# A two-layer hybrid encoder: table steps at even distances, and gate projections moved between the attention heads

## Chip, core and metric

The kernel runs on one core of a Trainium2 chip. TensorE (PE in the rows) multiplies, VectorE (DVE), ScalarE (ACT) and GpSimd (POOL) do the element-wise work, SyncE (SP) only issues transfers. Each engine works through its own instructions in order and waits for the others by semaphores. The metric is the device time of one execution, in microseconds (us).

## What is computed

T = 512 tokens, D = 1024, two layers, all in float32. Each layer is, cut to what matters here:

```python
h = rms_norm(x, norm_mix_g[i])
q, k, v, u_f, u_s, gates = split(h @ w_in[i])        # 8 heads of 128; gates: 3 x 1024
y_a = (rms_norm(diff_attention(q, k, v), subln) * c) @ w_attn_br[i]
y_b = fourier_mix(u_f) @ w_fourier_br[i]
z   = gelu(s5_mix(u_s, ...)) @ w_glu[i] + b_glu[i]   # s5: a diagonal state space, both directions
y_c = z[..., :D] * sigmoid(z[..., D:])
g   = sigmoid(gates)
x = x + (g[:, :D]*y_a + g[:, D:2*D]*y_b + g[:, 2*D:]*y_c) @ w_out[i]
h = rms_norm(x, norm_ffn_g[i]);  up = h @ w_up[i]
x = x + (gelu(conv3(up[:, :F])) * up[:, F:]) @ w_down[i]           # F = 22 * 128
x = x + sigmoid(rms_norm(x) @ w_ple_gate[i]) * (p[i] @ w_ple[i])
```

## The kernel before

Activations lie feature-major: a tile holds 128 features by 512 tokens (256 KB in float32). Every product keeps float32 accuracy by a split: each operand is a high part in a reduced format and a low part with the rest, and three matmuls (hi·hi, lo·hi, hi·lo) make one product (`mm`, L106). A weight matrix of 1024 x 128 is a "unit": SyncE loads 512 KB into `wr` (two buffers), ScalarE copies the high part into `wh` (L94), VectorE subtracts to get the low part `wl` (L95), and TensorE does 24 matmuls of 128x512 on it into one of the PSUM tiles `w`. One such unit, multiplied by 1/rms (L626) and put through tanh, is a gate tile (`gate`): m = 32 to 39 gate the attention branch, 40 to 47 the Fourier branch, 48 to 55 the S5 branch.

A layer (`i` = 0 is layer 1) is written as a sequence of stages, and a list scheduler turns the whole program into one instruction order for each engine: what is written first has priority, and what is written later moves ahead into places where an engine would wait. `tc.high_priority(offset=-LOW)` puts a part behind all the rest.

- Norm, then the projection of `u_s` to DRAM (`usd`) and the Fourier mixing.
- Eight heads: `v_pair` for every second head, `qk_proj` for q and k, and `head` (scores, softmax, transposes, product with v, in two halves of the queries; then the head's own norm). In layer 1 the tables of the S5 stage are made between them at low priority (`s5_tables`, one call for each of eight chunks): complex products on GpSimd (L243 to L248, L413 to L433), sums on VectorE (L415, L434), transposing matmuls on TensorE (L425) with copies on ScalarE, and the results go to DRAM (`tab`, `dtab`).
- Eight `s5_chunk`: load the chunk's tables `tb` (1.5 MB, two buffers, L660), 16 matmuls `pv` into `s` (L678), a chain over ScalarE, GpSimd and VectorE with a scan (L683 to L695) that leaves `z`, 24 matmuls `py` into `t` (L701 to L704), and a store of the result `ye` to DRAM (`ysd`). Behind the chunks the gates 32 to 39 and w_attn, then w_four with gates 40 to 47, then gates 48 to 55 (`gc8`) are written; the scheduler puts their matmuls between those of the chunks.
- `s5_out`: 32 loads of 32 KB from `ysd` into `yt` (L716), gelu, split into `soh` and `sol`. These feed w_glu (`s<-soh`), then the branches are merged and w_out follows.
- Feed-forward: 22 turns `f` of one unit "up" (L976, convolution, gelu) and one unit "gate" (product `uu` on GpSimd, L988), then eight output tiles `k` of w_down with 66 matmuls each (L1006). In layer 1 the tables of layer 2 are made here: `steps` is a generator with nine steps (`s5_steps`), and `next(steps)` writes one step, the GpSimd products of one chunk and the matmuls of the chunk before. Which turns call it is written out by hand.
- The gated per-layer embedding (PLE). Layer 2 has no table work; its tables were made in layer 1's feed-forward.

Of the kernel before, what the change touches and what calls it, by code (L numbers as in the profile page):

```python
# [21 lines left out]
L = 2  # L22
NH = 8
KT = 8
# [26 lines left out]
class Kernel:  # L51
# [504 lines left out]
        nc.scalar.activation(z[64:128, 1], ra[64:128], AF.Copy)  # L556
        return a, z

    def head(self, ap, q, k, v, e, nl, gs, bank="m"):

        nc = self.nc
        V = nc.vector
        kk, kl = k
        vh, vl = v
        o = self.ps("o")
        s1 = self.t(ap, "s1", (P, 4), bufs=2)
        s2 = self.t(ap, "s2", (P, 4), bufs=2)
        for half in range(2):
            hs = self.t(ap, "ath", (P, 4, 256), F32R, bufs=2)
            ls = self.t(ap, "atl", (P, 4, 256), F32R, bufs=2)  # L570
            for qi in range(2):
                qs = slice((half * 2 + qi) * P, (half * 2 + qi + 1) * P)
                mx = self.t(ap, "mx", (P, 2), bufs=3)
                qt = half * 2 + qi
                ss = []
                for c in range(2):
                    s = self.ps("s")
                    nc.tensor.matmul(s, lhsT=q[:, c, qs], rhs=kk[:, c], start=True, stop=False)
                    nc.tensor.matmul(s, lhsT=q[:, c, qs], rhs=kl[:, c], start=False, stop=True)  # L579
                    V.tensor_reduce(mx[:, c:c + 1], s, op=ALU.max, axis=AX.X, negate=True)  # L580
                    ss.append(s)
                pr = []
                for c in range(2):
                    pt = self.t(ap, f"pr{c}", bufs=2)
                    nc.scalar.activation(pt, ss[c], AF.Exp, bias=mx[:, c:c + 1],  # L585
                                         accum_out=(s1, s2)[c][:, qt:qt + 1])
                    pr.append(pt)

                c2 = self.t(ap, "c2", (P, 1), bufs=3)
                V.reciprocal(c2, s2[:, qt:qt + 1])  # L590
                V.tensor_scalar(out=c2, in0=c2, scalar1=s1[:, qt:qt + 1], scalar2=nl, op0=ALU.mult, op1=ALU.mult)
                V.scalar_tensor_tensor(out=pr[0], in0=pr[1], scalar=c2, in1=pr[0], op0=ALU.mult, op1=ALU.add)  # L592
                at = self.ps("t")
                for kt in range(4):
                    nc.tensor.transpose(at[:, kt * P:(kt + 1) * P], pr[0][:, kt * P:(kt + 1) * P], self.ident)
                self.split(at.rearrange("p (k q) -> p k q", k=4), hs[:, :, qi * P:(qi + 1) * P],
                           ls[:, :, qi * P:(qi + 1) * P])
            oh = o[:, half * 256:half * 256 + 256]
            n = 0
            for vv, aa in ((vh, hs), (vl, hs), (vh, ls)):  # L600
                for kt in range(4):
                    nc.tensor.matmul(oh, lhsT=vv[kt][:, e * P:(e + 1) * P],  # L602
                                     rhs=aa[:, kt],
                                     start=(n == 0), stop=(n == 11))
                    n += 1

        osb = self.t(ap, "osb", bufs=1)
        og = self.t(ap, "og", bufs=1)
        nc.scalar.activation(osb, o, AF.Square)
        nc.scalar.activation(og, o, AF.Copy)  # L610
        V.scalar_tensor_tensor(out=s1, in0=s1, scalar=EPS, in1=s1, op0=ALU.mult, op1=ALU.mult)
        _, pb = self.rms(osb, P, s1, bank)
        V.tensor_tensor(out=og, in0=og, in1=pb, op=ALU.mult)
        h = self.t(self.op, "oh", dt=F32R, bufs=NH)
        l = self.t(self.op, "ol", dt=F32R, bufs=NH)
        self.split(og, h, l, scale=gs)
        return h, l

    def gate(self, pool, i, m, hh, hl, rb):

        nc = self.nc
        w = self.unit(self.a["w_in"][i, m])
        ps = self.ps_w()
        self.mm(ps, w, hh, hl)
        ga = self.t(pool, "ga", bufs=4)
        nc.vector.tensor_tensor(out=ga, in0=ps, in1=rb, op=ALU.mult)  # L626
        nc.scalar.activation(ga, ga, AF.Tanh, scale=0.5)
        return ga


# [158 lines left out]
    def layer(self, i, x):  # L789
# [5 lines left out]
        hh, hl, rc, rb = self.norm(x, V_GMIX)  # L795
# [12 lines left out]
        nlam, gsub = self.t(rp, "nlam", (P, 1)), self.t(rp, "gsub", (P, 1))  # L808
# [30 lines left out]
        ap = self.pool(f"att{i}")  # L839

        kz = [self.t(aq, f"kz{n}", (P, 2, T), F32R) for n in range(2)]
        for z in kz:
            G.memset(z[64:128, 0].bitcast(F32), 0.0)
            G.memset(z[0:64, 1].bitcast(F32), 0.0)
        v = None
        oh, ol = [], []
        for h in range(NH):
            if h % 2 == 0:
                v = self.v_pair(i, ap, h // 2, hh, hl, rc)
            q = self.qk_proj(i, ar, aq, h, "q", hh, hl, cosr, sinr)  # L850
            k = self.qk_proj(i, ar, aq, 8 + h, "k", hh, hl, cosr, sinr, kz[h % 2])
            if i == 0:
                with tc.high_priority(offset=-LOW):
                    for ch in ([0, 1] if h == 0 else [h + 1] if h < 7 else []):
                        for _ in self.s5_tables(i, ch, "mmmm", tc.tile_snap_priority() - LOW):
                            pass
            r = self.head(ap, q, k, v, h % 2, nlam, gsub, "t" if h >= 7 else "m")
            oh.append(r[0])
            ol.append(r[1])
        if i == 0:  # L860
# [14 lines left out]
        for k in range(KT):  # L875
            ga = ga8[k]
# [14 lines left out]
        for k in range(KT):  # L891
            if k % 2 == 0:
                w = self.unit(a["w_four"][i, k // 2])
            ps = self.ps_w()
            self.mm(ps, w[(k % 2) * 4:(k % 2) * 4 + 4], fh, fl)
            ga = self.gate(ge if k < 4 else gt, i, 40 + k, hh, hl, rb)
            V.scalar_tensor_tensor(out=ga, in0=ga, scalar=1.0, in1=ps, op0=ALU.add, op1=ALU.mult)
            G.tensor_tensor(out=m[k], in0=m[k], in1=ga, op=ALU.add)
        gc8 = [self.gate(ge if k < 4 else gt, i, 48 + k, hh, hl, rb) for k in range(KT)]
        s5.release()  # L900
        sp = self.pool(f"so{i}")
        gl = self.pool(f"gl{i}")
# [68 lines left out]
        for f in range(NF):  # L971
# [14 lines left out]
            u = self.t(ff, "uu", bufs=2)  # L986
            V.tensor_tensor(out=u, in0=ps, in1=rb, op=ALU.mult)
            G.tensor_tensor(out=u, in0=u, in1=c, op=ALU.mult)  # L988
            if i + 1 < L and f in (8, 10, 13, 15, 18, 20):
                next(steps)  # L990
            h = self.t((fa, fb)[f // half], "ah", dt=F32R, bufs=half)
            l = self.t((fa, fb)[f // half], "al", dt=F32R, bufs=half)
# [3 lines left out]
        for k in range(KT):  # L996
            w = []
            for c in range(0, NF, 8):
                n = min(8, NF - c)
                w.append(self.unit(a["w_down"][i, k, :, c * P:(c + n) * P], cols=n * P))  # L1000
            ps = self.ps_w()
            c = 0
            for b, u in enumerate(w):
                self.mm(ps, u, ah[c:c + len(u)], al[c:c + len(u)], start=(b == 0), stop=(b == len(w) - 1))
                c += len(u)
            V.tensor_tensor(out=x[k], in0=ps, in1=x[k], op=ALU.add)  # L1006
            if i + 1 < L and k in (0, 1, 3):
                next(steps)
        fb.release()
        fa.release()  # L1010
# [267 lines left out]
```

## Time and profile before

| | |
|---|---|
| three runs | 2200.38, 2203.23 (median), 2203.36 us |
| profiled execution | 2204.09 us; its span from first to last instruction 2202.1 us |
| TensorE busy | 2104.7 us, 96% of the span |
| VectorE, ScalarE, GpSimd busy | 1499.7, 1014.8, 714.0 us |
| mean granted TensorE clock | 0.980 of full speed |

A busy TensorE is counted from the start of a matmul to its modelled end, and matmuls overlap, so what one matmul costs is read from long runs of them in the chain of waits. The granted clock of a stretch is a mean over its time: where the clock is low, the engine runs at 1.2 instead of 2.4 GHz. Where a view gives a line such as L106 for many matmuls, the tile names tell them apart (`w<-hh,wh` is a matmul of the weight's high part by the activation's high part `hh` into `w`).

### The profile page before, as it was taken

The page shows a single profiled execution, that of the slowest core. Times are in us where ns is not written, and L with a number is a line of the kernel's source. Part 1 is how long each engine was busy: PE and PEld are TensorE (multiplying, and loading weights), DVE is VectorE, ACT ScalarE, POOL GpSimd, SP SyncE. Part 2 cuts the span into 40 slices and gives each one's busy share as a digit, 9 for nine tenths or more (in the row PEclk, how much of TensorE's full clock was granted, in tenths as well). Part 3 has the DMA queues.
Part 4 walks back from the last instruction along what each step waited for, and adds up shares of the span by engine and source line. Part 5 has one row for each costly group of instructions (what it writes and reads, how often), then busy time and mean ns, then how long its engine had stood idle before and what let it go on. Part 6 is the DMA issues. An engine that isn't in the chain of part 4 may idle for free.

```text
span 2202.1 us, 28732 instructions
## 1 busy us (share of the span) xinstructions
PE 2104.7 (96%) x10432; PEld 1770.9 (80%) x10432; DVE 1499.7 (68%) x2497; ACT 1014.8 (46%) x1900; POOL 714.0 (32%) x618
## 2 busy tenths in 40 slices
PE   8799889899999999989999999999999999999998
PEld 6778778788888787777888988787888888888886
DVE  7988898366567988785467588764666666665344
ACT  4266656244434443333244577652444444444333
POOL 4488786023002337686112333201320011110000
PEclk9899999999999999989999999999999999999999
DMA  5233223765323244345534312126743333333341
GB/s 193 75 109 100 82 99 123 193 206 196 116 91 98 77 145 138 124 137 160 175 117 154 103 56 58 58 68 160 251 156 104 95 96 96 96 96 98 98 129 58
DMA packets 119038, 263.37 MB, mean 120 GB/s; under 512 B 44369, under 2 KB 50513, under 8 KB 116721
## 3 DMA queue, kind: packets, MB, share of 16 engines
q1 hardware_dynamic: 102672, 247.84, 35.6%
q10 hardware_dynamic: 16224, 13.70, 2.6%
q8 instruction: 82, 1.34, 0.2%
q14 instruction: 60, 0.48, 0.1%
HBM read 218.97 MB, written 42.47 MB: 119 GB/s over the span
## 4 chain that ended last, share of the span: by engine, by line
PE 65%; DVE 9%; POOL 5%; DMA 4%; ACT 3%; issue 1%; ACTq 0%; DVEq 0%; SPq 0%; POOLq 0%
PE w L106 49%; PE s L106 5%; DVE wl L95 2%; PE w L1139 1%; PE s L678 1%; DMA tab<-tb 1%; DMA U<-usd 1%; PE o L602 1%; DMA fraw<-fd 1%; PE w L1086 1%; PE w L1088 1%; PE w L1087 1%; PE t L704 1%; PE t L701 1%; PE t L702 1%
## 5 line engine op out<-in xcount | busy, mean ns | idle before, releaser
L95 DVE TENSOR_TENSOR wl<-wr,wh 128x512 fp32r<-128x512 f32 x596 | 478.6, 809 | 242.2 <-ACT wh L94 238.5
L106 PE MATMUL w<-hh,wh 128*128 128x512 f32 x1536 | 608.7, 397 | 23.4 <-DVE rs L538 7.7
L106 PE MATMUL w<-hl,wh 128*128 128x512 f32 x1536 | 605.1, 394 | 2.6 <-DVE hl L82 2.5
L106 PE MATMUL w<-hh,wl 128*128 128x512 f32 x1536 | 604.8, 394 | 0.0
L94 ACT ACTIVATE wh<-wr 128x512 fp32r<-128x512 f32 x596 | 365.2, 623 | 516.4 <-PE w L106 357.0
L106 PEld LDWEIGHTS w<-hh,wh 128*128 128x128 f32 x1536 | 291.8, 190 | 89.2 <-DVE rs L538 9.5
L106 PEld LDWEIGHTS w<-hl,wh 128*128 128x128 f32 x1536 | 291.8, 190 | 64.1 <-DVE hl L82 4.9
L106 PEld LDWEIGHTS w<-hh,wl 128*128 128x128 f32 x1536 | 291.2, 190 | 60.6 <-DVE wl L95 0.2
L988 POOL TENSOR_TENSOR uu<-uu,cv 128x512 f32<-128x512 f32 x44 | 70.5, 1602 | 287.6 <-DVE cv L198 287.6
L186 POOL TENSOR_TENSOR sq<-sq,sq 128x512 f32<-128x512 f32 x18 | 25.3, 1404 | 352.5 <-ACT sq L184 352.4
L106 PE MATMUL w<-ah,wh 128*128 128x512 f32 x352 | 138.5, 393 | 0.0
L106 PE MATMUL w<-ah,wl 128*128 128x512 f32 x352 | 138.2, 392 | 0.0
L106 PE MATMUL w<-al,wh 128*128 128x512 f32 x352 | 137.2, 390 | 0.0
L585 ACT ACTIVATE pr<-s,mx 128x512 f32<-128x512 f32 x128 | 88.0, 690 | 36.5 <-DVE mx L580 35.8
L580 DVE TENSOR_REDUCE mx<-s 128x1 f32<-128x512 f32 x128 | 85.6, 681 | 22.5 <-PE s L579 22.1
L539 POOL TENSOR_TENSOR rs<-rs,sinr 128x512 f32<-128x512 f32 x32 | 48.1, 1503 | 106.1 <-DVE rs L538 93.5
L112 POOL TENSOR_TENSOR rsq<-rmv,mhalf 128x4 f32<-128x4 f32 x22 | 25.6, 1166 | 169.1 <-DVE rmv L145 98.4
L106 PEld LDWEIGHTS w<-ah,wl 128*128 128x128 f32 x352 | 66.4, 189 | 14.7
L106 PEld LDWEIGHTS w<-al,wh 128*128 128x128 f32 x352 | 66.4, 189 | 14.1
L106 PEld LDWEIGHTS w<-ah,wh 128*128 128x128 f32 x352 | 66.4, 189 | 13.5
L106 PE MATMUL w<-oh,wh 128*128 128x512 f32 x128 | 51.8, 410 | 10.0 <-ACT wh L94 10.0
L592 DVE SCALAR_TENSOR_TENSOR pr<-pr,c,pr 128x512 f32<-128x512 f32 x64 | 59.7, 933 | 1.4
(422 smaller groups left out, 4152.7 us busy)
## 6 DMA issues: line engine op xcount, KB each, us to landing
wr<-in_w_in SPq DMA_DIRECT2D x112, 512.0 KB
wr<-in_w_up SPq DMA_DIRECT2D x88, 512.0 KB
tb<-tab SPq DMA_DIRECT2D x16, 1536.0 KB
tab<-tb SPq DMA_DIRECT2D x64, 256.0 KB
wr<-in_w_down SPq DMA_DIRECT2D x32, 512.0 KB
tab<-vbt SPq DMA_DIRECT2D x32, 256.0 KB
wr<-in_w_attn SPq DMA_DIRECT2D x16, 512.0 KB
wr<-in_w_glu SPq DMA_DIRECT2D x16, 512.0 KB
```

The source lines that it names most:

```text
L94: nc.scalar.activation(hi[:, :n], raw[:, c:c + n], AF.Copy)
L95: nc.vector.tensor_tensor(out=lo[:, :n], in0=raw[:, c:c + n], in1=hi[:, :n].bitcast(F32), op=ALU.subtract)
L106: nc.tensor.matmul(ps, lhsT=w[i][a], rhs=b[i], start=start and i == 0 and q == 0, stop=stop and i == n - 1 and q == 2)
L112: self.nc.gpsimd.tensor_tensor(out=y, in0=v, in1=self.mhalf[:, :n], op=ALU.pow)
L186: eng.tensor_tensor(out=sq, in0=sq, in1=acc[c], op=ALU.add)
L539: nc.gpsimd.tensor_tensor(out=rs, in0=rs, in1=sinr, op=ALU.mult)
L580: V.tensor_reduce(mx[:, c:c + 1], s, op=ALU.max, axis=AX.X, negate=True)
L585: nc.scalar.activation(pt, ss[c], AF.Exp, bias=mx[:, c:c + 1], accum_out=(s1, s2)[c][:, qt:qt + 1])
L592: V.scalar_tensor_tensor(out=pr[0], in0=pr[1], scalar=c2, in1=pr[0], op0=ALU.mult, op1=ALU.add)
L602: nc.tensor.matmul(oh, lhsT=vv[kt][:, e * P:(e + 1) * P], rhs=aa[:, kt], start=(n == 0), stop=(n == 11))
L678: nc.tensor.matmul(pv[:, c0:c0 + NC], lhsT=tb[:, d, g * P:(g + 1) * P], rhs=u, start=True, stop=True)
L988: G.tensor_tensor(out=u, in0=u, in1=c, op=ALU.mult)
```

## The change

Two things. First, the turns of the feed-forward loop that call `next(steps)`: six turns and three output tiles become five turns and four output tiles. Second, in layer 1 alone, the 16 gates 40 to 55 are no longer computed behind the heads. `gate_out` computes gate 40 + 2h ahead of head h and gate 41 + 2h between the halves of head h, in the one buffer that the head's squared output `osb` also uses, and stores the tile to DRAM (`gd`) on ScalarE's queue. Where the gate is used, `gate_in` loads it back into a `ga` tile on SyncE's queue. Gates 32 to 39 and all of layer 2 stay.

```diff
-    def head(self, ap, q, k, v, e, nl, gs, bank="m"):
+    def head(self, ap, q, k, v, e, nl, gs, bank="m", between=None):
@@ end of the loop over the two halves
+            if half == 0 and between is not None:
+                between()
@@ gate
-    def gate(self, pool, i, m, hh, hl, rb):
+    def gate(self, pool, i, m, hh, hl, rb, tag="ga", bufs=4):
...
-        ga = self.t(pool, "ga", bufs=4)
+        ga = self.t(pool, tag, bufs=bufs)
...
+    def gate_out(self, pool, i, m, hh, hl, rb):
+        ga = self.gate(pool, i, m, hh, hl, rb, "osb", 1)
+        self.gd[m] = self.t(self.dp, f"gd{m}")
+        self.nc.scalar.dma_start(self.gd[m], ga)
+
+    def gate_in(self, pool, i, m, hh, hl, rb):
+        if m not in self.gd:
+            return self.gate(pool, i, m, hh, hl, rb)
+        ga = self.t(pool, "ga", bufs=4)
+        self.nc.sync.dma_start(ga, self.gd[m])
+        return ga
@@ loop over the heads
-            r = self.head(ap, q, k, v, h % 2, nlam, gsub, "t" if h >= 7 else "m")
+            if i == 0:
+                self.gate_out(ap, i, 40 + 2 * h, hh, hl, rb)
+            r = self.head(ap, q, k, v, h % 2, nlam, gsub, "t" if h >= 7 else "m",
+                          (lambda: self.gate_out(ap, i, 41 + 2 * h, hh, hl, rb)) if i == 0 else None)
@@ merging
-            ga = self.gate(ge if k < 4 else gt, i, 40 + k, hh, hl, rb)
+            ga = self.gate_in(ge if k < 4 else gt, i, 40 + k, hh, hl, rb)
...
-        gc8 = [self.gate(ge if k < 4 else gt, i, 48 + k, hh, hl, rb) for k in range(KT)]
+        gc8 = [self.gate_in(ge if k < 4 else gt, i, 48 + k, hh, hl, rb) for k in range(KT)]
@@ feed-forward
-            if i + 1 < L and f in (8, 10, 13, 15, 18, 20):
+            if i + 1 < L and f in (7, 10, 13, 16, 19):
                 next(steps)
...
-            if i + 1 < L and k in (0, 1, 3):
+            if i + 1 < L and k in (0, 2, 4, 6):
                 next(steps)
```

How this moves the instructions is seen in the engines' orders. TensorE at the last chunk of layer 1's S5 stage (`s<-U` is `pv`, `t<-z` and `t<-U` are `py`, `w<-hh` a gate), before:

```order
L678 MATMUL s_4405<-U_4051,tb_4396 128x64 x8
L106 MATMUL w_5444<-hh_114,wh_5436 128x512
L106 MATMUL w_5444<-hl_115,wh_5436 128x512
L702 MATMUL t_4380<-z_4366,tb_4348 128x63
L704 MATMUL t_4380<-z_4366,tb_4348 128x63
L701 MATMUL t_4380<-U_4051,dr_4352 128x64
L702 MATMUL t_4380<-z_4366,tb_4348 128x63
L704 MATMUL t_4380<-z_4366,tb_4348 128x63
L701 MATMUL t_4380<-U_4051,dr_4352 128x64
L702 MATMUL t_4380<-z_4366,tb_4348 128x63
L704 MATMUL t_4380<-z_4366,tb_4348 128x63
L701 MATMUL t_4380<-U_4051,dr_4352 128x64
```

and in the changed kernel, where line 678 is 693 and lines 701, 702 and 704 are 716, 717 and 719:

```order
L717 MATMUL t_4972<-z_4958,tb_4940 128x63
L719 MATMUL t_4972<-z_4958,tb_4940 128x63
L693 MATMUL s_4997<-U_4691,tb_4988 128x64 x8
L716 MATMUL t_5020<-U_4691,dr_4992 128x64
L693 MATMUL s_5045<-U_4691,tb_5036 128x64 x8
L717 MATMUL t_5020<-z_5006,tb_4988 128x63
L719 MATMUL t_5020<-z_5006,tb_4988 128x63
L716 MATMUL t_5020<-U_4691,dr_4992 128x64
L717 MATMUL t_5020<-z_5006,tb_4988 128x63
L719 MATMUL t_5020<-z_5006,tb_4988 128x63
L716 MATMUL t_5020<-U_4691,dr_4992 128x64
L717 MATMUL t_5020<-z_5006,tb_4988 128x63
```

Between the last two `pv` and behind them there were gate and w_four matmuls; now the chunks' own matmuls stand one after the other. In the whole stretch from the first `pv` to the first `s<-soh`, 528 matmuls of 128x512 have become 193.

ScalarE in the heads, at the norm of the second head's output (`osb`, `og`), before:

```order
L81 ACTIVATE vh_1949<-w_1824,rsq_179 128x256
L609 ACTIVATE osb_1799<-o_1672 128x512
L610 ACTIVATE og_1800<-o_1672 128x512
L426 ACTIVATE vbt_1636<-m_1637 128x256
L427 ACTIVATE kfb_986<-m_1637 128x32
L78 ACTIVATE ath_2116<-t_2135 128x4x128
L585 ACTIVATE pr_505_2189,s_482_2114<-s_2181,mx_2180 128x512
L81 ACTIVATE vh_1953<-w_1824,rsq_179 128x256
L81 ACTIVATE vh_2689<-w_2571,rsq_179 128x256
```

and in the changed kernel (L609 is L611; L629 is a gate's tanh):

```order
L611 ACTIVATE osb_1959<-o_1792 128x512
L612 ACTIVATE og_1960<-o_1792 128x512
L94 ACTIVATE wh_2510<-wr_2504 128x512
L81 ACTIVATE vh_2113<-w_1984,rsq_179 128x256
L94 ACTIVATE wh_2552<-wr_2550 128x512
L94 ACTIVATE wh_2556<-wr_2550 128x512
L629 ACTIVATE osb_2308<-osb_2308 128x512
L636 DMA gd_520_2311<-osb_2308 128x512
L544 ACTIVATE ks_2204<-ra_2198 128x1024
```

A gate's weight copies (L94), its tanh and its store to `gd` have come in behind the head's `osb`, in the same buffer.

ScalarE at the end of layer 1's feed-forward (`dtab` is the last table, `hh` the activation for the next stage, one tile for each output tile `x0` to `x7`), before:

```order
L491 DMA dtab_1484_6692<-kfb_1474_6681 48x512
L491 DMA dtab_1484_6692<-kfb_1474_6681 32x512
L491 DMA dtab_1484_6692<-kfb_1474_6681 16x512
L81 ACTIVATE hh_2191_10181<-x4_1312_5923,vec_7_86 128x512
L94 ACTIVATE wh_2152_9949<-wr_2149_9943 128x512
L78 ACTIVATE ph_2213_10245<-praw_2212_10243 128x512
L94 ACTIVATE wh_2155_9955<-wr_2154_9953 128x512
L78 ACTIVATE ph_2216_10251<-praw_2215_10249 128x512
L94 ACTIVATE wh_2157_9959<-wr_2154_9953 128x512
L94 ACTIVATE wh_2160_9965<-wr_2159_9963 128x512
L94 ACTIVATE wh_2162_9969<-wr_2159_9963 128x256
L81 ACTIVATE hh_2193_10185<-x5_1313_5924,vec_7_86 128x512
```

and in the changed kernel:

```order
L94 ACTIVATE wh_2259_10342<-wr_2256_10336 128x512
L94 ACTIVATE wh_2265_10385<-wr_2264_10383 128x512
L491 DMA dtab_1516_6756<-kfb_1506_6745 128x512
L491 DMA dtab_1516_6756<-kfb_1506_6745 112x512
L491 DMA dtab_1516_6756<-kfb_1506_6745 96x512
L491 DMA dtab_1516_6756<-kfb_1506_6745 80x512
L491 DMA dtab_1516_6756<-kfb_1506_6745 64x512
L491 DMA dtab_1516_6756<-kfb_1506_6745 48x512
L491 DMA dtab_1516_6756<-kfb_1506_6745 32x512
L491 DMA dtab_1516_6756<-kfb_1506_6745 16x512
L81 ACTIVATE hh_2229_10257<-x7_1347_5990,vec_7_86 128x512
```

The `dtab` transfers, which stood ahead of the fifth of the eight `hh`, now stand ahead of the eighth.

## Rows read from the trace of the kernel before

**Rows 1.** the page: busy time by engine; costliest groups, one of them

```profile
PE 2104.7 (96%) x10432; PEld 1770.9 (80%) x10432; DVE 1499.7 (68%) x2497; ACT 1014.8 (46%) x1900; POOL 714.0 (32%) x618
...
L988 POOL TENSOR_TENSOR uu<-uu,cv 128x512 f32<-128x512 f32 x44 | 70.5, 1602 | 287.6 <-DVE cv L198 287.6
```

**Rows 2.** the chain of waits, pieces in order: start us, us, what

```profile
415.40 15.55 DMA U<-usd
...
476.42 1.73 PE s L678 x16
...
501.78 1.79 PE s L678 x16
...
1786.74 346.21 PE w L106 x1522
```

**Rows 3.** stretches: length, busy of PE, PEld, DVE, ACT, POOL, clock, DMA share

```profile
100.00:400.00 300.00, 276.22 (x1562) 238.22 (x1562) 252.69 (x414) 181.48 (x395) 219.58 (x186) 0.97 0.32 106
400.00:446.00 46.00, 38.77 (x168) 31.32 (x166) 14.51 (x25) 10.91 (x20) 1.40 (x2) 0.89 0.82 186
446.00:602.00 156.00, 156.00 (x848) 134.70 (x846) 98.17 (x134) 72.73 (x120) 37.85 (x31) 1.00 0.54 176
1245.00:1500.00 255.00, 249.53 (x1437) 215.91 (x1436) 186.55 (x354) 166.03 (x325) 68.43 (x50) 1.00 0.20 64
```

**Rows 4.** TensorE's waits from 100 to 400 us: total, times, longest

```profile
PE w L106 <- DVE rs L538: 7.0, 3, 3.4
PE m L425 <- DVE tb L415: 3.8, 1, 3.8
```

**Rows 5.** TensorE's waits from 700 to 1106 us

```profile
PE m L425 <- DVE tb L415: 18.6, 3, 7.9
```

**Rows 6.** the feed-forward stage and a stretch in it, columns as in rows 3

```profile
700.00:1106.00 406.00, 381.21 (x1690) 315.07 (x1690) 307.36 (x467) 153.07 (x302) 219.91 (x181) 0.96 0.42 135
880.00:892.00 12.00, 6.35 (x22) 5.67 (x23) 9.24 (x9) 3.10 (x6) 10.77 (x9) 0.57 0.35 109
```

**Rows 7.** first and last mark of the feed-forward stage, layer 1, then 2

```profile
L976 DVE TENSOR_TENSOR gp<-w,rstd x22: 672/679/687, 708.5 to 970.4; 128x512 f32<-128x512 f32 x22
...
L1006 DVE TENSOR_TENSOR x<-w,x x8: 672/682/692, 992.4 to 1105.0; 128x512 f32<-128x512 f32 x8
...
L976 DVE TENSOR_TENSOR gp<-w,rstd x22: 678/693/694, 1787.4 to 2006.7; 128x512 f32<-128x512 f32 x22
...
L1006 DVE TENSOR_TENSOR x<-w,x x8: 690/692/692, 2027.2 to 2133.0; 128x512 f32<-128x512 f32 x8
```

**Rows 8.** the table matmuls: one of four banks; two neighbours in time

```profile
L425 PE MATMUL m<-cat,tb x32: 283/286/580, 816.4 to 1043.3; 128*128 128x144 f32 x32
...
816.36 0.65 PE L425 MATMUL m<-cat,tb 128*128 128x144 f32 x4
816.84 0.65 PE L425 MATMUL o<-cat,tb 128*128 128x144 f32 x4
```

**Rows 9.** VectorE by line, 120 to 360 us, then 2000 to 2100 us

```profile
L95 DVE TENSOR_TENSOR wl<-wr,wh 128x512 fp32r<-128x512 f32 x35 | 42.5, 1224 | 7.5 <-ACT wh L94 7.4
...
L95 DVE TENSOR_TENSOR wl<-wr,wh 128x512 fp32r<-128x512 f32 x33 | 22.9, 693 | 54.3 <-ACT wh L94 54.2
```

**Rows 10.** loads of tb (440 to 560 us); a chunk's first, last link

```profile
L660 SPq DMA_DIRECT2D tb<-tab x6: 326/327/589, 466.8 to 527.3; - x6
...
503.66 0.59 ACT L683 ACTIVATE sw<-s 64x512 f32<-64x512 f32 x1 [1.39 <-PE s L678]
...
511.98 0.68 DVE L695 TENSOR_TENSOR z<-z,sw 128x512 f32<-128x512 f32 x1
```

**Rows 11.** tiles yt, sol and soh from 540 to 640 us

```profile
L716 SPq DMA_DIRECT2D yt<-ysd x32: 574/575/698, 552.6 to 578.3; - x32
...
L106 PE MATMUL s<-soh,wh x53: 387/394/397, 601.5 to 639.8; 128*128 128x512 f32 x53
L82 DVE SCALAR_TENSOR_TENSOR sol<-yg,soh x4: 1089/1098/1106, 568.1 to 585.4; 128x512 fp32r<-128x512 f32 x4
```

More of the change, by code (lines that the diff above doesn't have):

```diff
@@ L845, in layer @@
         v = None
+        self.gd = {}
         oh, ol = [], []
```

## Prediction

> **What bounds the kernel now.** I read the busy table first, then the table by stage, the chain of waits, and TensorE's waits in the stages that the change touches. TensorE is busy 2104.7 of 2202.1 us [rows 1], and one 128x512 matmul of the long runs takes 346.21/1522 = 0.227 us [rows 2]: a 1024x128 projection ("unit", 24 such matmuls) takes 5.45 us. So time can only come from stretches in which TensorE idles or runs at the lower clock, and these are few. In layer 1's attention (100 to 446 us) TensorE idles 23.8 + 7.2 us, and at granted clocks of 0.97 and 0.89 it does about 9 + 5 us less than at full clock: 45 us lost [rows 3]. Layer 2's heads, without table work, lose 5.5 us in 255 [rows 3]. The waits in layer 1 are for VectorE, which in turn follows GpSimd's chains [rows 4], and the stage closes on transfers, the last of them the 15.55 us gather of U [rows 2]. The second place is layer 1's feed-forward stage: from its first to its last mark on VectorE it takes 1105.0 - 708.5 = 396.5 us, layer 2's 2133.0 - 1787.4 = 345.6 us [rows 7]. Of the 50.9 us difference the table matmuls themselves explain 15 (four banks of 32, four matmuls in 816.84 - 816.36 = 0.48 us [rows 8], so 128 x 0.12); 35 are lost: 24.8 idle in 406 us, the rest low clock [rows 6]. The S5 chunk stage (446 to 602) has TensorE full, 156.00 of 156 [rows 3].
>
> **Part 1: table steps in the feed-forward stage.** Nothing is added: nine calls of `next(steps)` stay nine. Over the stage GpSimd is busy 219.91 us [rows 6], of which 22 products `uu` at 1.6 us [rows 1] are 35; the other 185 are eight chunks of tables at 23. With three `uu` beside it a chunk takes 28 us, some 31 with the waits inside its chain. Before, the steps follow each other after 2, 3, 2, 3, 2 turns of up and gate; a turn is two units, 10.9 us of TensorE work, so every other step comes after 21.8, less than GpSimd's 31, and TensorE waits for `tb` 18.6 us in three waits [rows 5]. Around one of them, in 880 to 892, the granted clock is 0.57 [rows 6]. After: every third turn (32.7 us), then every second output tile of w_down (2 x 66 x 0.227 = 30). I take the waits for `tb` as gone, with the lower clock behind them: 32 of the 35 us. What is late next: the last step now comes at k = 6. Its chain (table matmuls, ScalarE's copies, 15 `dtab` transfers on ScalarE's queue) stands ahead of the copy of the last `hh` that the next stage needs, where before four more output tiles' work covered it. I put 5 us on that (0: the 66 matmuls of k = 7, 15 us, cover it; 12: most of the chain's transfers are open). Sum: -32 + 5 = -27 us, bounds -15 (half of the waits stay, since the margins are within 2 us) and -33.
>
> **Part 2: 16 gates moved into the heads.** It takes 16 units from behind the heads and puts them among the heads: 16 x 5.45 = 87 us of TensorE work, none saved. It adds 16 stores of 256 KB on ScalarE's queue and 16 loads on SyncE's, and the weights' 512 KB loads move along. In the attention the DMA engines are busy 0.32 of the time [rows 3], so I cost these at nothing; if that cover were gone, the loads would delay the `tb` behind them on SyncE's queue, which belongs to the second rival.
>
> Heads. In the order, 193 matmuls of 128x512 stand between the first chunk and the first `soh` matmul, where 528 stood: 335 x 0.227 = 76 us of work come ahead of the first chunk and may fill holes. Of the 45 us lost, layer 2's level over 346 us (5.5 x 346/255 = 7.5) is the least that stays: recovery at most 37. At least 10: each unit also needs VectorE (two subtractions, one product, 0.7 us each at best), which is busy 252.69 of 300 us [rows 3], and no unit shortens the transfers at the stage's end. I take 28: GpSimd's 219.58 us would spread over some 350 us instead of 300, a share of 63% instead of 73%, so that its chains are late less often. First chunk: 76 - 28 = 48 us later.
>
> On VectorE the subtraction `wl` takes 1224 ns in the heads, beside GpSimd, and 693 ns late in layer 2, where GpSimd hardly works [rows 9]. The Trainium skill (SBUF — State Buffer, "Who interferes with whom") says that a VectorE instruction with two SBUF inputs contends with a GpSimd instruction that reads SBUF, and that whichever comes second is blocked until the other is through. By that rule, with which the two rows agree, 32 subtractions moved beside GpSimd's tables would cost 32 x 0.53 = 17 us, in part on GpSimd's chains; the third rival has this as a mechanism of its own.
>
> Chunk stage. Before, it is full of work: 528 x 0.227 = 120 us and the chunks' own. A chunk has 16 `pv` matmuls (1.73 us [rows 2]) and 24 `py` matmuls of that size (2.6 us): 35 us for eight. After, 193 x 0.227 + 35 = 79 us are left, and the chunks' chain sets the pace. `tb` has two buffers, so chunk n+2 loads only after chunk n's last matmul. One cycle: the load of `tb` at most 476.42 - 466.8 = 9.6 us [rows 2, 10]; from the start of `pv` to `z` 512.66 - 501.78 = 10.9 [rows 2, 10]; `py` 2.6: 23. Measured for a cycle of two chunks, with other work between the links: 501.78 - 476.42 = 25.4 [rows 2]. From first `pv` to last `py` it was 552.6 - 446 = 107 us [rows 3, 11]. Without other work in the way three cycles of 20 (a load of 6.5, my guess) and 23 for the two ends give 83; between 83 and 107 I take 97, the measured being nearer. Then `s5_out`: 32 loads of `yt` from 552.6 to 578.3, and the last `sol` 8 us later (585.4 + 1.1) [rows 11]: 34 us. After, the 32 stand together on SyncE (32 x 0.575 = 18 us of issue), and most need early chunks alone; between 17 and 34 I take 24. Some `soh` matmuls are through by then (-4), the clock has to come back after holes (+3): 97 + 24 - 1 = 120 us against 156: -36. Before, the gates covered `s5_out`'s 34 us and 15 more up to 601.5 [rows 11]; that cover is gone.
>
> Layer 1 up to the feed-forward: +48 - 36 = +12 (ends: -28, all filled; +35, least recovery and old pace). From the end of layer 1's feed-forward on the order is the same.
>
> **Sum.** +12 - 27 = -15 us on the profiled execution's 2204.09: 2189. The median of the runs is 0.9 us below the profiled execution: 2188.
>
> **Rivals.**
> 1. The fill suffices: no chunk stalls, the stage falls to its 79 us of work: +48 - 76 - 27 = -55, 2148 us. For it: w_attn units stand among the first chunks. Against: in the order the last four chunks have next to nothing between them. 0.11.
> 2. Slower: the chunk chain keeps its old pace without its filler, 107 + 34 = 141 us from first `pv` to the last `sol`, and the heads recover only 16: +60 - 15 - 27 = +18, 2221 us. For it: 25.4 us is nearly the sum of the links with a load of 9.6. With 28 recovered it decides once the stretch passes 135 us (48 - (156 - 135) - 27 = 0). 0.15.
> 3. VectorE and GpSimd hold each other up in the heads: each moved subtraction blocks for its 0.69 us, 32 x 0.69 = 22 of the 28 us recovered are lost: +7, 2210 us. For it: the two means [rows 9]. Against: the rest of the heads' units bear the same already. 0.10.
> 4. Even spacing gains nothing, since GpSimd's 31 us is an average and its chain also waits for transfers: +12 alone, 2215 us. Against: the waits are few, three, and at short distances. 0.04.
>
> **How the numbers follow.** The forecast has 0.60, its own range 2172 to 2206: part 1 between -15 and -33, layer 1 between +2 and +18. The whole range, 2162 to 2216, leaves out rival 1 and the upper part of rival 2. A difference of 0.2% (4.4 us) is about what a measurement of this kernel can tell from no change. Faster: 0.49 of the forecast's 0.60 and rival 1's 0.11, 0.60. Same: 0.08 of the forecast and 0.04 of rival 3, 0.12. Slower: rivals 2 and 4, the rest of 3 and 0.03 of the forecast, 0.28.
>
> **What would show it.** Right: layer 1's feed-forward marks some 27 us closer, hardly a wait for `tb` there; first `pv` near 494 us; TensorE idle 30 to 45 us in the chunk stage, waiting for `z` and for `soh`; first `pv` to first long run of `soh` matmuls near 120 us. Wrong: a chunk stage with TensorE full (rival 1) or over 135 us long (2); a first `pv` after 510 us (3); unchanged waits for `tb` (4).

## The result, and the profile after

The changed kernel is slower: 2234.23 us median (2232.45 to 2235.95) against 2201.92, ratio 1.0146 with a 95% interval of 1.0133 to 1.0158. Forecast was 2188, with a range up to 2216. The profiled execution has a span of 2233.1 us, 31.0 more than before. (Ratios here and below compare runs in the chip's faster state; of all the runs one, of `e11_dummy` below, was not in it: 3051.58 us at a granted clock of 0.651.) First the page: total busy time, and the 40 slices of TensorE's busy share and granted clock.

```profile
PE 2123.8 (95%) x10432; PEld 1776.5 (80%) x10432; DVE 1488.9 (67%) x2497; ACT 1013.8 (45%) x1900; POOL 714.3 (32%) x618
PE   8899999999779999999999999999999999999998
PEclk9899999999679999999999999999999999999999
```

In the 11th and 12th slice (558 to 670 us) TensorE is busy at 7 tenths and the granted clock falls to 6 and 7 tenths: the second half of layer 1's S5 chunk stage and the `soh` matmuls behind it; TensorE was full there before. The table by stage (length, busy of PE, PEld, DVE, ACT, POOL, clock, DMA share):

```profile
100.00:460.00 360.00, 343.02 (x1850) 289.02 (x1849) 270.61 (x456) 204.89 (x436) 221.94 (x186) 0.99 0.37 122
460.00:506.00 46.00, 44.21 (x202) 36.26 (x201) 14.45 (x24) 12.29 (x21) 1.13 (x2) 0.96 0.78 182
506.00:641.60 135.60, 105.34 (x539) 90.09 (x537) 74.71 (x93) 48.30 (x80) 38.49 (x31) 0.78 0.54 179
740.00:1140.00 400.00, 382.66 (x1710) 313.42 (x1709) 303.52 (x450) 153.80 (x302) 217.19 (x181) 0.99 0.43 136
```

Against [rows 3]: from 100 us to the first `pv` it is now 406 us instead of 346, with 18.8 us idle instead of 31. The stage from 506 on is 30 us idle at a clock of 0.78. The marks that bound the stages, by tile and line (the two `soh` numbers come from the chain of waits, next block):

```profile
L693 PE MATMUL s<-U,tb x128: 217/275/472, 505.9 to 600.9; 128*128 128x64 f32 x128
...
L719 PE MATMUL t<-z,tb x64: 275/348/422, 521.9 to 614.5; 128*128 128x63 f32 x64
...
L995 DVE TENSOR_TENSOR gp<-w,rstd x22: 674/680/687, 744.3 to 1001.4; 128x512 f32<-128x512 f32 x22
...
L1025 DVE TENSOR_TENSOR x<-w,x x8: 672/676/692, 1018.3 to 1129.9; 128x512 f32<-128x512 f32 x8
...
L995 DVE TENSOR_TENSOR gp<-w,rstd x22: 680/693/694, 1818.5 to 2037.7; 128x512 f32<-128x512 f32 x22
```

And the chain of waits (start us, us, what):

```profile
480.36 14.30 DMA U<-usd
590.51 7.09 DMA tb<-tab
597.64 3.64 PE s L693 x16
...
641.60 28.84 PE s L106 x120
```

The same marks before, first `pv`, last `py` and the long run of `soh` in the chain:

```profile
L678 PE MATMUL s<-U,tb x128: 217/275/276, 445.5 to 539.0; 128*128 128x64 f32 x128
...
L704 PE MATMUL t<-z,tb x64: 275/275/275, 461.2 to 552.4; 128*128 128x63 f32 x64
...
601.69 32.98 PE s L106 x144
```

These marks account for the difference (the feed-forward marks of before stand in [rows 7]):

| stage of layer 1 | before | after | difference | forecast |
|---|---|---|---|---|
| up to the first `pv` | 445.5 | 505.9 | +60.4 | +48 |
| first `pv` to the long run of `soh` matmuls | 156.2 | 135.7 | -20.5 | |
| from there to the first feed-forward mark | 106.8 | 102.7 | -4.1 | -36 with the row above |
| feed-forward, first to last mark | 396.5 | 385.6 | -10.9 | -32 |
| from there to layer 2's first feed-forward mark | 682.4 | 688.6 | +6.2 | +5 |
| sum | | | +31.1 | -15 |

Every gain that was forecast came with the right sign, but smaller: 16 us in the heads for 28, 25 in the chunk stage for 36, 11 in the feed-forward for 32. Of the 46 us between forecast and result, the feed-forward is 21, the heads 12, the chunk stage 11 and the end of the feed-forward 1. What TensorE waits for now, in the heads (100 to 460), the chunk stage (505 to 645) and the feed-forward (730 to 1150), total us, times, longest:

```profile
PE s L578 <- ACT pr L585: 8.3, 13, 1.4
...
PE s L106 <- ACT soh L81: 14.8, 4, 8.8
PE t L717 <- DVE z L710: 8.6, 4, 3.6
PE s L693 <- DMA tb<-tab: 3.8, 1, 3.8
...
PE w L106 <- DVE gp L995: 9.6, 5, 4.9
PE w L106 <- ACT ge L197: 2.9, 2, 1.6
PE w L106 <- ACT ah L81: 2.5, 1, 2.5
```

The feed-forward's 18.6 us for `tb` [rows 5] is gone, as forecast, and the three waits shown last, 15.0 us, stand there instead. Two of them were there before as well, with 3.3 us (`gp` 1.8, `ge` 1.5); all of TensorE's waits between the first and the last mark fall from 24.6 us to 15.8. The longest, in order of time, on GpSimd, VectorE and TensorE (start us, us, engine, line; in brackets the idle time before it and what ended it):

```profile
911.72 1.51 POOL L247 TENSOR_TENSOR tb<-pt 128x512 f32<-128x512 f32 x1
913.31 1.63 POOL L248 TENSOR_TENSOR tb<-tb,tb 128x512 f32<-128x512 f32 x1
...
917.14 1.05 POOL L414 TENSOR_TENSOR tb<-pt,bc 128x512 f32<-128x512 f32 x1
918.15 1.26 POOL L1007 TENSOR_TENSOR uu<-uu,cv 128x512 f32<-128x512 f32 x1
...
911.53 0.78 DVE L198 SCALAR_TENSOR_TENSOR cv<-ge,cv 128x512 f32<-128x512 f32 x1
...
918.23 1.73 DVE L415 TENSOR_TENSOR tb<-tb,tb 128x512 f32<-128x512 f32 x1 [2.75 <-POOL tb L414]
920.11 1.31 DVE L82 SCALAR_TENSOR_TENSOR al<-uu,ah 128x512 fp32r<-128x512 f32 x1
921.35 0.68 DVE L995 TENSOR_TENSOR gp<-w,rstd 128x512 f32<-128x512 f32 x1
...
922.17 0.76 PE L106 MATMUL w<-hh,wh 128*128 128x512 f32 x1 [4.87 <-DVE gp L995]
```

The gelu's result `cv` is there at 912.3 (911.53 + 0.78), but the product `uu` starts on GpSimd at 918.15, behind the table products L247 to L414 in its queue. `al` on VectorE follows it, `gp` stands behind `al` in VectorE's queue and frees TensorE's PSUM tile only at 922: 4.87 us idle. But ahead of `al` in VectorE's queue stands a table sum (L415), which waits 2.75 us for GpSimd's L414 and ends at 919.96, while `al` has its operands at 920.08 (ScalarE's copy `ah` of `uu`): without the late `uu`, `al` would have begun only some 0.15 us earlier. So here two results of GpSimd's queue are late together, and the table sum alone would have held `gp`. The same order, L414, L415, `al`, `gp`, stands ahead of the waits for `gp` that end at 882 and 962.

### The profile page after: what moved, and what is told of

It is laid out like the page before. It is cut to its first block, busy times and chain, and to the rows that moved or that the text cites. A ratio compares the mean times of both kernels' runs of the same rounds, so it can differ in the third digit from the quotient of the medians.

```text
span 2233.1 us, 28798 instructions
## 1 busy us (share of the span) xinstructions
PE 2123.8 (95%) x10432; PEld 1776.5 (80%) x10432; DVE 1488.9 (67%) x2497; ACT 1013.8 (45%) x1900; POOL 714.3 (32%) x618
## 4 chain that ended last, share of the span: by engine, by line
PE 69%; DVE 11%; POOL 7%; DMA 5%; ACT 4%; issue 3%; SPq 1%; ACTq 1%; DVEq 0%; POOLq 0%
PE w L106 50%; PE s L106 5%; PE w L1158 3%; DVE wl L95 2%; PE o L602 1%; PE s L693 1%; DMA U<-usd 1%; DMA tab<-tb 1%; PE s L578 1%; PE s L579 1%; PE t L595 1%; PE t L719 1%; PE t L717 1%; POOL uu L1007 1%; PE w L1105 1%
## 5 line engine op out<-in xcount | busy, mean ns | idle before, releaser
L95 DVE TENSOR_TENSOR wl<-wr,wh 128x512 fp32r<-128x512 f32 x596 | 470.9, 796 | 238.7 <-ACT wh L94 235.6
L94 ACT ACTIVATE wh<-wr 128x512 fp32r<-128x512 f32 x596 | 364.5, 622 | 494.6 <-PE w L106 348.5
L106 PEld LDWEIGHTS w<-al,wh 128*128 128x128 f32 x352 | 66.1, 188 | 14.6 <-DVE al L82 0.5
L106 PE MATMUL s<-soh,wh 128*128 128x512 f32 x128 | 51.5, 408 | 15.2 <-ACT soh L81 14.8
L578 PE MATMUL s<-ks,qs 128*128 128x512 f32 x128 | 54.3, 432 | 10.0 <-ACT pr L585 9.6
```

Of the source, the lines that this page charges most:

```text
L94: nc.scalar.activation(hi[:, :n], raw[:, c:c + n], AF.Copy)
L95: nc.vector.tensor_tensor(out=lo[:, :n], in0=raw[:, c:c + n], in1=hi[:, :n].bitcast(F32), op=ALU.subtract)
L106: nc.tensor.matmul(ps, lhsT=w[i][a], rhs=b[i], start=start and i == 0 and q == 0, stop=stop and i == n - 1 and q == 2)
```

## The experiments

All are timed against the kernel before on the same chip. Where stage times are given, they are read from the same marks as in the table above.

**The two parts alone.** `e1_spacing` is the kernel before with the two lines of the feed-forward changed; `e2_gates16` is the changed kernel with these two lines put back.

> The kernel before with the new table turns alone (gates stay behind the heads). Theory S, the two parts add up stage by stage as the marks of the changed kernel say: feed-forward marks of layer 1 closer by 11 us (385.6 instead of 396.5), then 6 us lost again up to layer 2, so 5 us less than before, 2197. Rival: the part of the changed kernel's feed-forward that is still lost comes from what the moved gates did before it, and the spacing alone brings the full 27 us, 2175. Second rival: the spacing brings nothing by itself, 2202.

> The changed kernel with the old table turns: the 16 gates alone. Theory S: first pv 60 us later, first pv to the long soh run 20 us shorter, 4 us won behind it: 36 us more than before, 2238. Rival: the gates cost less than that and the turns cost part of the 31 us: under 2225.

Measured: 2195.72 us, ratio 0.997 (0.9962 to 0.9979), and 2241.78, ratio 1.0177 (1.0164 to 1.0191). Together -0.3% and +1.8% make the +1.5% of both, so the parts add up, theory S. The spacing is worth 7 us, the gates cost 39.

How far marks of two single executions can be told apart: in `before`, `e1_spacing`, `e4_uu` and `e8_uu_old`, whose code up to the first `pv` is the same, it starts at 445.5, 443.8, 442.7 and 441.5 us. A difference of 4 us at that mark therefore shows little.

**How many gates, and where.** `e3_gates8` moves eight, one ahead of each head, with the old turns:

```diff
-                self.gate_out(ap, i, 40 + 2 * h, hh, hl, rb)
+                self.gate_out(ap, i, 40 + h, hh, hl, rb)
...
-                          (lambda: self.gate_out(ap, i, 41 + 2 * h, hh, hl, rb)) if i == 0 else None)
+                          None)
```

> Eight gates (40 to 47, one ahead of each head) pass through DRAM instead of 16, the eight gates 48 to 55 stay behind w_four; old table turns. Theory H, the heads have few holes that a gate fits into, so about a fifth of the moved work is recovered, and the chunk chain keeps its 107 us whatever filler it has: first pv later by 35 (8 x 5.45 less a fifth), the stage from first pv to the soh run 135 to 141 us instead of 156: 15 to 20 us more than before, 2217 to 2222. Rival C, the loss is the starved chunk stage alone: eight gates are enough filler for s5_out's 34 us, the heads fill their holes (28 of 44 us recovered): same as before or faster, 2190 to 2202.

Measured: 2214.28 us, ratio 1.0051 (1.0036 to 1.0066), between the two forecasts and nearer to H's. The first `pv` comes 23.8 us later (469.3). How much work has moved ahead of it is counted as in the prediction, by the matmuls that start before it. From the start to the first `pv`, before, here and in `e2_gates16` (columns as in the table by stage, matmuls in the first bracket):

```profile
0.00:445.40 445.40, 392.34 (x2116) 334.50 (x2117) 350.43 (x650) 229.24 (x492) 270.77 (x253) 0.95 0.40 122
```

```profile
0.00:469.20 469.20, 425.34 (x2284) 358.88 (x2285) 356.79 (x669) 241.41 (x513) 269.35 (x253) 0.98 0.41 129
```

```profile
0.00:506.20 506.20, 464.53 (x2451) 389.96 (x2452) 370.72 (x694) 254.87 (x536) 273.81 (x253) 0.98 0.42 131
```

Eight gates are 43.6 us of work, but 24 matmuls of w_attn that ran ahead of the first `pv` before now come behind it: 168 more matmuls, 38.1 us at 0.227. So 14 us are recovered (the work moved ahead less the delay), more than H's fifth and less than C's two thirds. With 16 gates it is 335 matmuls, 76 us, for 60.8 us, 15 recovered: the second eight added about nothing. From the first `pv` to the long run of `soh` matmuls it takes 146.0 us (615.3 - 469.3), 10 less than before (theory H: 15 to 21), and to the first feed-forward mark 14 less. The eight chunks themselves, first `pv` to last `py`, take 118.6 us, longer than the 107 that H wanted to stay; why they are longer stays open:

```profile
L693 PE MATMUL s<-U,tb x128: 217/275/276, 469.3 to 572.7; 128*128 128x64 f32 x128
...
L719 PE MATMUL t<-z,tb x64: 275/275/421, 483.9 to 587.9; 128*128 128x63 f32 x64
```

`e5_between8` puts the same eight between the halves, `e9_ahead16` all 16 ahead of the heads, two at a time; both with the old turns.

> Eight gates (40 to 47) again, but each between the halves of its head instead of ahead of it; old table turns. With the eight ahead of the heads the first pv came 24 us later for 43.6 us of moved work; with all 16 it came 61 later for 76. Theory P, the place: a gate between the halves recovers nothing, it only lengthens the head: first pv 36 to 44 us later than before, total 12 to 20 us over the run with eight ahead, 2226 to 2234. Rival N, the number: the heads hold some 20 us of room whatever the place, and eight gates use it up: first pv again about 24 us later, total 2212 to 2217.

> All 16 gates, two ahead of each head and none between its halves; old table turns. Theory P: first pv 48 us later than before or less (half of 76 recovered, and more), total below 2230. Rival N: first pv about 60 us later as in the changed kernel, total 2238 to 2243.

Measured: 2223.03, ratio 1.0101 (1.0087 to 1.0114), first `pv` 28.5 us later; and 2239.27, ratio 1.0173 (1.0159 to 1.0187), first `pv` 58.7 later. With eight gates the first `pv` lies between the two theories and nearer to N, with 16 it is as N says. The work moved ahead is again 168 matmuls in the one and 328 in the other, so 10 and 16 us are recovered. So it is mainly the number: the heads have room for 10 to 16 us. The place shows 5 us at this mark with eight gates and 2 with 16, about what marks of single executions scatter. In the whole time the eight between the halves are 10 us slower than the eight ahead (6 above N's range, 3 below P's), which the first `pv` explains only in part; with 16 the place makes no difference.

**GpSimd's queue in the feed-forward.** `e4_uu` is `e1_spacing` with layer 1's products `uu` on VectorE, `e8_uu_old` the same edit with the old turns:

```diff
-            G.tensor_tensor(out=u, in0=u, in1=c, op=ALU.mult)
+            (V if i + 1 < L else G).tensor_tensor(out=u, in0=u, in1=c, op=ALU.mult)
```

> As the run with the new turns alone, and layer 1's 22 products uu go to VectorE instead of GpSimd. Theory Q, in the changed kernel the products uu wait behind the table products in GpSimd's queue, al behind them and gp behind al on VectorE, so TensorE's waits for gp, ge and ah (15 us) go with this: 8 to 12 us less than the new turns alone, about 2187. Rival V, VectorE itself is the bound there (304 of 400 us busy): 22 x 0.7 = 15 us more on it, no gain or a loss against the new turns alone, 2197 to 2210.

> The kernel before with uu of layer 1 on VectorE alone, old turns. Theory Q: uu waits in GpSimd's queue with either table of turns, but with the old turns TensorE waits for the table matmuls' tb first (18.6 us), which needs GpSimd's speed; GpSimd has 35 us less to do, so part of this goes too: 5 to 10 us less than before, 2192 to 2197. Rival: without uu on GpSimd the old turns are as good as the new ones, 2180 to 2185. Second rival: no change, 2202.

Measured: 2182.50 us, ratio 0.9912 (0.9899 to 0.9926), and 2190.28, ratio 0.9956 (0.9944 to 0.9969). Theory Q holds: 13 us less than the new turns alone, although VectorE has more to do. With the old turns the edit gives 11, a little over what Q expected. The new turns are worth 9 us on top of this edit, each against its own runs of the kernel before, and were worth 7 without it. The waits of TensorE in the new turns without and with the edit (700 to 1110 us, total, times, longest):

```profile
PE w L106 <- DVE gp L976: 7.5, 5, 2.8
PE w L106 <- ACT ge L197: 4.5, 3, 1.6
PE w L106 <- ACT ah L81: 2.5, 1, 2.5
```

```profile
PE w L106 <- DVE gp L976: 6.4, 4, 2.6
```

The waits for `ge` and `ah` are gone and that for `gp` hardly less (7.5 to 6.4), which theory Q had wrong in part; the marks from first to last are 372.0 us apart instead of 386.6. VectorE's own waits in the same stretch, without and with the edit, show both halves:

```profile
DVE tb L415 <- POOL tb L414: 26.0, 8, 7.3
DVE al L82 <- ACT ah L81: 17.2, 14, 2.0
```

```profile
DVE tb L415 <- POOL tb L414: 32.8, 8, 8.6
...
DVE al L82 <- ACT ah L81: 0.9, 2, 0.7
```

The wait of `al` for `ah`, ScalarE's copy of `uu`, is gone: that was the late `uu`. The table sums L415 still wait for GpSimd, and the two longest waits for `gp` that are left, 2.6 and 2.5 us, end behind such sums in VectorE's queue. Between the two marks TensorE idles 6.5 us instead of 16.4.

**What paces the chunks.** In `e2_gates16`, with hardly any filler, first `pv` to last `py` took 109 us, in the kernel before 107. Two runs start from `e2_gates16` (all 16 gates moved, old turns). `e10_halftb` loads half of each table and has four buffers for it; the products with the other half take the first half's rows instead, so this kernel leaves that part of the result out:

```diff
-        tb = self.t(pool, "tb", (P, 6, 512), bufs=2)
-        nc.sync.dma_start(tb, tab.rearrange("p (k x) -> p k x", k=6))
+        tb = self.t(pool, "tb", (P, 3, 512), bufs=4)
+        nc.sync.dma_start(tb, tab.rearrange("p (k x) -> p k x", k=6)[:, 0:3])
...
```

`e11_dummy` adds 42 matmuls that keep TensorE running:

```diff
+        if self.gd and ch < 7:
+            with self.tc.high_priority(offset=-LOW):
+                dm = self.ps("o")
+                for r in range(6):
+                    nc.tensor.matmul(dm, lhsT=U[:, 0:2].rearrange("p g c -> p (g c)"),
+                                     rhs=U[:, 0:8].rearrange("p g c -> p (g c)"), start=True, stop=True)
```

> All 16 gates moved, old table turns, and each chunk loads half of its table (0.75 MB; the second half of the products uses the first half's rows, so this part of the result is left out) into four buffers instead of two, so that no load waits for an earlier chunk. With 16 gates moved the stage takes 109 us from first to last chunk. Theory L, the load of tb behind the chunk before last is what keeps the chain at its old pace: 85 to 92 us, total 2218 to 2225. Rival K, it is the low clock after TensorE has run out of filler, which doubles the chunk's own matmuls: still over 100 us, total 2233 to 2241.

> All 16 gates moved, old table turns, and 42 added matmuls in layer 1's chunk stage whose result nobody reads, six for each of seven chunks at low priority, so that TensorE is not idle between the chunks' links. Theory K: the clock stays near 1.00 up to the last chunk, the chunks' own matmuls keep their 1.7 and 2.6 us, and the stage falls from 109 to 95 to 100 us although there is more to do; total 2228 to 2234. Rival L: the chunks wait for tb as before and the added matmuls stand in the way: 109 us or more, total 2241 to 2255.

Measured: 2224.69 us, ratio 1.0097 (1.008 to 1.0113), and 2252.58 (the middle one of three), ratio 1.0225 (1.0208 to 1.0242). First `pv` and last `py` with half tables, and then with added matmuls (count, duration in ns min/median/max, first and last start):

```profile
L693 PE MATMUL s<-U,tb x128: 218/275/422, 508.3 to 560.1; 128*128 128x64 f32 x128
...
L719 PE MATMUL t<-z,tb x64: 275/275/421, 523.4 to 580.3; 128*128 128x63 f32 x64
```

```profile
L693 PE MATMUL s<-U,tb x128: 218/275/276, 504.0 to 603.9; 128*128 128x64 f32 x128
...
L725 PE MATMUL t<-z,tb x64: 275/275/275, 521.8 to 620.3; 128*128 128x63 f32 x64
```

And the table by stage of the run with added matmuls (columns as above), with the time that the added matmuls take:

```profile
506.00:560.00 54.00, 54.00 (x273) 39.53 (x272) 26.41 (x38) 17.98 (x31) 13.31 (x12) 1.00 0.55 179
560.00:615.00 55.00, 55.00 (x277) 41.89 (x277) 28.44 (x36) 18.87 (x33) 21.09 (x16) 1.00 0.64 214
...
L699 PE MATMUL o<-U 128*128 128x512 f32 x84 | 38.9, 597 | 0.0
```

Without the wait for a table, the eight chunks take 72 us (580.3 - 508.3) instead of 109: theory L, and by more than expected (bytes and buffers changed together here; `e12_split8` below keeps the bytes). At full clock with the added matmuls they take 116. This run doesn't settle what the clock is worth: TensorE is busy all of the time between 506 and 615, 38.9 us of it with the added matmuls, and these with the 79 us of the prediction's count fill the 116 us by themselves. What it shows is that this way of holding the clock cost more than it gave back, 11 us against `e2_gates16`. That a clock of 1.00 does not by itself make the chain quicker is seen in the kernel before, which took 107 us at 1.00 [rows 3], with other work between the links.

**Three gates, and a table in parts.** `e7_three` is `e4_uu` with gates 53 to 55 moved ahead of the third, fifth and seventh head. `e12_split8` is `e4_uu` with gates 40 to 47 ahead of the heads and each table in three tiles, of the same size in sum, whose buffers come free one by one; `e13_split` is `e4_uu` with these tiles alone:

```diff
-        tb = self.t(pool, "tb", (P, 6, 512), bufs=2)
-        nc.sync.dma_start(tb, tab.rearrange("p (k x) -> p k x", k=6))
+        tv = tab.rearrange("p (k x) -> p k x", k=6)
+        tb, tw, tc_ = [self.t(pool, n, (P, 2, 512), bufs=2) for n in ("tb", "tw", "tc")]
+        nc.sync.dma_start(tb, tv[:, 0:2])
+        nc.sync.dma_start(tc_, tv[:, 4:6])
+        nc.sync.dma_start(tw, tv[:, 2:4])
...
```

The tile `tb` now serves `pv`, `tc` the rotation in the chain, and `tw` `py`.

> The new turns, uu of layer 1 on VectorE, and three gates (53 to 55, ahead of heads 3, 5 and 7) moved instead of 16. Theory M, from first pv to the last sol the chunk chain needs 134 to 144 us whatever filler it has, and the kernel before has 15 us of gate work more than that behind it: three gates (16.4 us) can leave the chunk stage without uncovering s5_out, and the heads recover about half of them: 5 to 9 us less than the run without moved gates (2182.5), 2174 to 2178. Rival: the scheduler spends the remaining gates among the chunks and uncovers the end of s5_out anyway, 2182 or more.

> New turns, uu on VectorE, gates 40 to 47 ahead of the heads, and each chunk's table in three tiles of two matrices with two buffers each (same bytes, same memory), so that the parts for pv and for the rotation can be loaded while an earlier chunk still holds its py part. Theory L: the load's wait goes as with half tables, the chain from first pv to last py falls to 75 to 95 us and the stage with 112 us of work from 156 to about 125; the heads recover 20 of 44 us: 2173 to 2180, below the 2182.5 of the run without moved gates. Rival: three loads a chunk on SyncE's in-order queue stand in each other's way, and the stage stays at 140 or more: 2190 to 2200.

> The control: new turns and uu on VectorE, no gate moved, tables in three tiles. TensorE is full in the chunk stage, so the split alone brings nothing: 2180 to 2185, as without it (2182.5). Rival: the loads in three parts disturb the order of both layers' stages, 2186 or more.

Measured: `e7_three` 2184.61, ratio 0.9925 (0.9912 to 0.9939), no gain over `e4_uu`: the first `pv` comes 14.6 us later than there, for 48 more matmuls ahead of it (10.9 us; the gates are 16.4, but a unit of w_attn has gone behind). So nothing is recovered, where theory M had half, while the end of the stage was not uncovered. `e12_split8` 2177.63, ratio 0.989 (0.9875 to 0.9904), the fastest of all and as theory L had it; `e13_split` 2193.64, ratio 0.9959 (0.9946 to 0.9972), slower than without the tiles. Its chunks are through in 82 us as well (440.1 to 522.4), with all of the old filler beside them, but without moved gates nothing needs that. Its profiled execution is 7.5 us longer than that of `e4_uu`; from the first `pv` to the first `soh` matmul it takes 163.2 us instead of 156.3, in which TensorE idles 3.1 us instead of none and the granted clock is 0.98 instead of 1.00. Why TensorE stalls there stays open. The rows of `e12_split8` (L696 is `pv`, L722 the last of `py`):

```profile
L696 PE MATMUL s<-U,tb x128: 217/275/423, 469.9 to 522.0; 128*128 128x64 f32 x128
...
L722 PE MATMUL t<-z,tw x64: 275/275/275, 486.9 to 551.7; 128*128 128x63 f32 x64
...
L82 DVE SCALAR_TENSOR_TENSOR sol<-yg,soh x4: 1093/1098/1116, 565.6 to 583.0; 128x512 fp32r<-128x512 f32 x4
```

Here eight gates, 43.6 us, have left the stage (and one unit of w_attn has come in), its chain takes 551.7 - 469.9 = 82 us, and the last `sol` at 584 is again ahead of the first `soh` matmul at 593. The first feed-forward mark comes 5.6 us earlier than in `e4_uu` (700.2 against 705.8). Each of the two has its own runs of the kernel before; the intervals of their ratios overlap by 0.0005, so the 5 us between them are likely, not certain. Against `e3_gates8`, with the same gates in the same places, the tiles take the chunks from 118.6 to 82 us; against `e4_uu`, with none moved, `e13_split` takes them from 107 to 82. In both pairs bytes and memory are the same, and the other edits of `e12_split8` lie behind this stage, so what changes the pace is that each part of a table is loaded and released by itself.

## Why the prediction was wrong, step by step

**Which stretches lose time.** Right for the heads and the low clock. Wrong for the feed-forward: "35 are lost" took the difference of marks on VectorE as TensorE's. Layer 1's fourth mark stands 33.7 us behind the first (742.2), layer 2's 23.4 (1810.8), before any table matmul and in both kernels, while TensorE is without a gap longer than half a microsecond in these turns. So a part of the 35 us, 10 by this reading, was a late first mark in layer 2. `e4_uu` gets 24.5 us out of this stage and still idles 6.5 in it, so 31 were there to be had.

**"I take the waits for `tb` as gone": right; "32 of the 35 us": the step that failed here.** The prediction asked what comes late next only at the end of the stage. Inside it GpSimd's queue holds both the tables and `uu`, at any spacing. Where `uu` comes late it holds ScalarE's copy `ah` and with it `al`; where a table product comes late it holds VectorE's sum L415; and `gp`, which frees TensorE's PSUM tile, stands behind both in VectorE's queue. TensorE's waits fell from 24.6 to 15.8 us only. Forecast -32, measured -10.9; with `uu` off that queue (`e4_uu`) the same stage gives -24.5, and what is left is 6.4 us for `gp`. The 5 us put on the last step at k = 6 came as 6.2.

**"I take 28" recovered in the heads: measured 76 - 60.4 = 15.6.** The bounds (10 to 37) held, the value in them was mis-sized. GpSimd's chains are late less often, as argued: the waits for `rs` and `tb`, 10.8 us in [rows 4], are 0.3 us now, idle time falls from 31 to 19 us and the clock rises to 0.99. What takes their place is the softmax, 8.3 us for ScalarE's `pr` in 13 waits (3.7 in 3 before). `e3_gates8`, `e5_between8` and `e9_ahead16` show a room of 10 to 16 us that eight gates use up.

**"between 83 and 107 I take 97": measured 109, above the upper end.** "Without other work in the way" the chain was to be quicker; the load of `tb`, which starts behind the last `py` two chunks earlier, kept the pace, as `e10_halftb`, `e12_split8` and `e13_split` show (72, 82 and 82 us), and the chunks' own matmuls took twice their time at the low clock (the last 16 `pv` 3.64 us at 597.64, where 1.73 stand in [rows 2]); whether that adds to the 109 was not separated. The load itself, put at 6.5 us as a guess, took 7.1 where the chain shows it (590.51). `s5_out` was right: from the last `py` to the last `sol` 25 us for 24. So the second rival's mechanism is what happened: the chain kept its old pace, and the heads recovered 15.6 where it had 16. Its time was 2221; the 13 us more are 22 us that the feed-forward and its end fell short by (-4.7 for -27), less 10 that the stage gave beyond the rival's -15.

**The other rivals.** The third: in the stretch of [rows 9], 120 to 360 us, the subtraction `wl` takes 911 ns on average instead of 1224, with GpSimd busy 166 of 240 us instead of 195; up to 420 us it is 974 (row below). So the gates met GpSimd less, not more. The Trainium skill's rule (SBUF — State Buffer, "Who interferes with whom"), that of two instructions which need the shared ports the second blocks, is not contradicted by this: it speaks of instructions that meet, GpSimd's work is spread over a longer stage here, and the subtraction is shorter where GpSimd is busy less. The blocking cost was not measured by itself. The first and the fourth rival did not come.

```profile
L95 DVE TENSOR_TENSOR wl<-wr,wh 128x512 fp32r<-128x512 f32 x58 | 56.0, 974 | 11.8 <-ACT wh L94 11.6
```

## What to carry to other kernels

A stage that is full because filler covers a dependent chain can only shrink to the length of that chain, so before filler is moved out, take the chain's measured pace, loads that wait for a buffer's release included, as the stage's new length. Moving work into holes recovers only what the holes hold (here 10 to 16 us, with eight gates or 16), so move that much and no more, and shorten the chain first (`e12_split8`). When a wait goes, look through the queue of the engine that caused it for everything else that stands there, since the next wait is likely to come from the same queue.

## What was not expected of the hardware

A wait behind one buffer release counts more than bytes alone would say: with the same bytes and memory in three tiles the chunks went from 118.6 to 82 us with eight gates moved, and from 107 to 82 with none; halving the tables and doubling the buffers took them from 109 to 72. Keeping TensorE at a clock of 1.00 by 38.9 us of added matmuls cost 11 us on balance.
